# A third expert with a fixed place in a streamed mixture of experts, and overflow rounds that load through one buffer of their own

## The chip, the cores and the metric

The kernel runs on one core of a Trainium2 chip. The metric is the device time of one execution, in microseconds. Below, TensorE is PE, VectorE is DVE, ScalarE is ACT, GpSimd is POOL, and SyncE, which here only issues DMAs, is SP; "SPq" or "PEq" is the sequencer of an engine, which runs its branches, register loads and DMA issues.

## The reference

A decoder trunk of two layers on 256 tokens of width 1024, in float32. Each layer is an attention block (layer 0: two groups of sparse heads; layer 1: latent attention beside sliding-window attention) and then a top-2 mixture of 16 experts of hidden width 512. Each block is normalised and modulated by a vector from `c`. A final RMSNorm follows. The part that the change touches is the mixture of experts:

```
for each token: the router picks 2 of 16 experts and their weights w
y[token] = sum over its 2 experts e of  w * ( silu(h @ gate[e]) * (h @ up[e]) ) @ down[e]
x = x + gate_vector * y
```

`gate[e]` and `up[e]` are 1024 x 512, `down[e]` is 512 x 1024. One expert's weights are 6 MB, those of one layer 96 MB.

## The kernel before

**Groups.** The 16 experts of a layer are worked through in seven groups of 128 slots (`GROUPS`). A group holds two or three places, and a place is one to three blocks of 32 slots for one expert. PE multiplies 128 slots at a time, so a group costs it about the same whether it has two or three experts, but a group of three loads 18 MB and one of two 12 MB. `(0, 3)` means place 0 with 96 slots. Experts 14 and 15 have fixed places in group 0. The other 14 experts are put into places 0 to 13 by their token count (`RANKS`, `SORTED`): the fullest experts go to the widest places. The result of this sort is `ex_p`, a row of expert numbers on the chip.

**Loads.** Every expert's gate, up and down matrices come as two loads of 1 MB each (gate 2, up 2, down 2), all issued on SP, 96 in a layer. They go into 15 buffers of 1 MB: a ring of 10 (`slot`) and 5 more that are free in this part of the program (`room`); a buffer is free again when PE has done its last matmul from it. Each SP load uses one of eight semaphores in turn and waits for the load eight before it, so at most eight are in flight. `load_both` loads group 0 (L1185), `load_experts` the other groups (L1171). From group 1 on, SP first reads the expert's number from `ex_p` into a register (`load_value`, L1349), so no load of a sorted expert is issued before the sort is done. At that point 12 buffers hold four loads of the modulation weights and the eight gate and up loads of group 0, and three buffers are empty.

**Order.** For each group the loop calls `hidden` (loads gate and up, and multiplies), then `rows` of the group before it (loads its down and multiplies), then the gathering of the next group's tokens. So PE's order, and SP's, is gate and up of group i, down of group i-1, gate and up of group i+1.

**Overflow.** Tokens that don't fit their expert's place are done in extra rounds of 64 slots, up to seven, ahead of group 3 (`rest`, `round_`). A nest of conditions (`tc.If(n >= i + 1)`, L1453) skips the rounds that aren't needed. PE, ACT, DVE and SP take part in this nest. A round's six loads go on SP into six of the ring's slots, which `rest` withholds from the stream. Since SP is held by the nest, the twelve loads of group 3 are issued on POOL's own queue (`self.after`), and group 2's down is loaded ahead of the nest. In the profiled execution no instruction of a round ran.

At the ends of the nest SP has eight UNCONDITIONAL_BRANCH, and seven of them wait for the eight load semaphores, that is for nearly all loads in flight.

Of the kernel before, what the change touches and what calls it, by code (L numbers as in the profile page):

```python
# [10 lines left out]
F32 = mybir.dt.float32  # L11
# [6 lines left out]
ET = mybir.EngineType  # L18
# [3 lines left out]
S, D, P = 256, 1024, 128  # L22
NE, DE = 16, 512
CAP = 64
# [3 lines left out]
RING, EXTRA = 10, 5  # L28


GROUPS = [[(14, 2), (15, 2)], [(0, 3), (1, 1)], [(2, 2), (3, 1), (4, 1)], [(5, 2), (6, 2)], [(7, 2), (8, 1), (9, 1)],
          [(10, 2), (11, 2)], [(12, 2), (13, 2)]]
RANKS = 0, 9, 1, 10, 11, 2, 3, 4, 12, 13, 5, 6, 7, 8
SORTED = len(RANKS)
BLOCK = 32

# [71 lines left out]
def trunk(ctx, tc, ins, out):  # L108
    nc = tc.nc
    mm, vec, act, pool, sp = nc.tensor.matmul, nc.vector, nc.scalar, nc.gpsimd, nc.sync  # L110
# [28 lines left out]
    def slot(n_k, n):  # L139

        tag = order.pop(0)
        order.append(tag)
        t = room() if tag == "wx" else ring.tile([P, 2048], F32, tag="w", name="slot")
        return t[:, :n_k * n].rearrange("p (k f) -> p k f", k=n_k)
# [822 lines left out]
    def moe(cp, wk, layer, norm, end):  # L967
# [9 lines left out]
        for t in range(2):  # L977
            at = slice(t * P, (t + 1) * P)
# [179 lines left out]
            split_rows(v, yg, vec)  # L1158
            return [yg[:, 0], yg[:, 1]]

        def load_experts(nm, experts, k, tiles=None, queue=sp, fine=False):

            out = [[] for _ in experts]
            for h in range(2):
                for i, e in enumerate(experts):
                    t = tiles.pop(0) if tiles else slot(4, 512)
                    v = ins[nm][layer][bass.ds(e, 1)].rearrange("o (p k) f -> p (o k) f", k=k)
                    n = k // 2
                    t = t.rearrange("p a b -> p (a b)").rearrange("p (k f) -> p k f", k=n)
                    if not (fine and h):  # L1170
                        queue.dma_start(t, v[:, n * h:n * h + n, :])  # L1171
                    out[i].append((t, n))
            for k0 in range(0, n if fine else 0, 2):
                for x, e in zip(out, experts):
                    v = ins[nm][layer][bass.ds(e, 1)].rearrange("o (p k) f -> p (o k) f", k=k)
                    queue.dma_start(x[1][0][:, k0:k0 + 2, :], v[:, n + k0:n + k0 + 2, :])
            return [Rows(x) for x in out]

        def load_both(nm, e0):
# [31 lines left out]
        class Group:  # L1211


            def __init__(self, i, o, XG, c0):
                self.first, self.last = i == 0, (layer, i) == (1, len(GROUPS) - 1)
                self.after = i == 3
                self.o, self.XG, self.c0 = o, XG, c0
                self.p0, self.n = GROUPS[i][0][0], len(GROUPS[i])
                self.parts = blocks(GROUPS[i])
                first = sum(len(g) for g in GROUPS[:i])  # L1220
                self.owner = const("owner")[:, first:first + self.n]
                es = list(range(self.p0, self.p0 + self.n))
                if i:
                    es = [load_value(ex_p[:, e:e + 1], [(ET.SP, ET.Pool)[self.after]], NE - 1) for e in es]
                self.es = es
                self.Wd = None

            def hidden(self):
                names = ("moe_w_gate", "moe_w_up")
                if self.first:  # L1230
                    W = [load_both(nm, self.p0) for nm in names]
                else:
                    W = [load_experts(nm, self.es, 8, queue=(sp, pool)[self.after], fine=self.last and nm == names[1])
                         for nm in names]
                self.hid = gate_up(self.XG, self.c0, self.parts, *W)

            def slots(self):
                self.OT = wk.tile([P, 2, P], F32R, tag="OT", name="OT")
# [12 lines left out]
            def load_down(self):  # L1251
                if self.Wd is not None:
                    return
                if not self.last:
                    self.Wd = load_experts("moe_w_down", self.es, 4, queue=(sp, pool)[self.after])
                    return

                src = [ins["moe_w_down"][layer][bass.ds(e, 1)].rearrange("o (p k) f -> p (o k) f", k=4) for e in self.es]
                self.Wd = []
                for sl, step in zip(end.pieces, (2, 4, 2)):  # L1260
                    n = sl.stop - sl.start
                    if n == 512:
                        tiles = [slot(4, n) for _ in range(2)]
                    else:
                        tile_ = slot(8, n)
                        tiles = [tile_[:, 0:4], tile_[:, 4:8]]
                    for k in range(0, 4, step):
                        for t, v in zip(tiles, src):
                            sp.dma_start(t[:, k:k + step], v[:, k:k + step, sl])
                    self.Wd.append(tiles)  # L1270
# [31 lines left out]


        NR = 7
        w_x = cp.tile([P, 1], F32, name="w_x")
        OT_x = cp.tile([P, 2, 2, P], F32R, name="OT_x")
        sides = [slice(0, 64), slice(64, 128)]

        def x_hidden(XG, W):
            hid = XG.rearrange("p k s -> p (k s)")[:, 0:256]  # L1310
            g, u = bank("mm", [P, 256]), bank("sc", [P, 256])
            for w, b in zip(W, (g, u)):
                for k in range(8):
                    for h, at in enumerate(sides):
                        mm(b[at], XG[:, k, :], w[k][:, 256 * h:256 * h + 256], start=k == 0, stop=k == 7)
            act.activation(hid, g, AF.Silu)
            vec.tensor_tensor(hid, u, hid, ALU.mult)
            return hid
# [18 lines left out]
        def x_down(hT, Wd):  # L1337
            v, yg = row_tiles()
            y = bank("o", [P, 512])
            for k in range(4):  # L1340
                for h, at in enumerate(sides):
                    mm(y[at], hT[:, k, :], Wd[k][:, 512 * h:512 * h + 512], start=k == 0, stop=k == 3)
            for h, at in enumerate(sides):
                vec.scalar_tensor_tensor(v[at], y[at], w_x[at], gate[at, 512 * h:512 * h + 512], ALU.mult, ALU.mult)
            split_rows(v, yg, vec)
            return [lambda h=h: combine(OT_x[:, h], [yg[:, 0], yg[:, 1]], slice(512 * h, 512 * h + 512)) for h in range(2)]

        def load_value(at, engines, top):
            _, v = nc.values_load_multi_w_load_instructions(  # L1349
                at, engines=engines, min_val=0, max_val=top, skip_runtime_bounds_check_because="sums of indicators")  # L1350
            return v[0]
# [34 lines left out]
        def rounds():  # L1386
# [42 lines left out]
                of(at_x[:, t], pos[:, t])  # L1429
            vec.tensor_tensor(at_x, at_x, skip.unsqueeze(1).to_broadcast([P, 2, NR]), ALU.subtract)  # L1430

        def round_(i, space, o, XG):

            e = load_value(ex_x[:, i:i + 1], [ET.SP], NE - 1)
            tiles = list(space)
            W = [load_experts(nm, [e], 8, tiles)[0] for nm in ("moe_w_gate", "moe_w_up")]
            Wd, = load_experts("moe_w_down", [e], 4, tiles)
            pick(o, at_x[:, :, i:i + 1].to_broadcast([P, 2, 2]), CAP)
            gather(XG, CAP, o)
            hid = x_hidden(XG, W)  # L1440
            x_slots(o, wt_x[:, :, i:i + 1])
            for f in x_down(x_transposed(XG, hid), Wd):
                f()

        def rest():
            space = [slot(4, 512) for _ in range(6)]
            o = pick_tile()[:, :, 0:2 * CAP]
            XG = hp.tile([P, 8, CAP], F32, tag="HT", name="XG")
            n = load_value(ex_x[:, NR:NR + 1], [ET.PE, ET.Activation, ET.DVE, ET.SP], NR)

            def go(i):
                if i < NR:
                    with tc.If(n >= i + 1):  # L1453
                        round_(i, space, o, XG)
                        go(i + 1)
            go(0)

# [6 lines left out]
        for i in range(len(GROUPS)):  # L1464
            p = Group(i, o, XG, 128 * (i > 0 and i % 2 == 0))
            if i == 3:
                before.load_down()
                flush()
                rest()
            if p.last:  # L1470
                end.load()
            p.hidden()
            if before is not None:
                before.rows()
            p.slots()
            p.turn()
            if i % 2 == 0 and i < 5:
                o, XG = gathered(*then)
            elif i < 5:
                then = picked([i + 2, i + 3], placed[:, 0:2])  # L1480
            if i == 0:
                rounds()
            flush()
            before = p
# [293 lines left out]
```

## Time and profile before

| | us |
|---|---|
| median of 3 runs (lowest to highest) | 868.07 (867.78 to 868.67) |
| profiled execution | 869.42 |
| its span on the core | 867.2 |
| PE busy | 746.6 (86%) |
| DVE busy | 377.8 (44%) |
| ACT busy | 237.4 (27%) |
| POOL busy | 115.6 (13%) |
| DMA traffic | 291.14 MB, mean 336 GB/s |

The profile lists the busy time of each engine, of which PE has the most, and the mean rate of DMA. The rate is not even: the page's row of 40 slices shows 415 to 422 GB/s in most slices of the two expert parts (about 233 to 468 us and 620 to 850 us) and 96 to 387 in the attention parts. The views used below are windows (busy time, granted clock and DMA rate of a stretch), waits (what an engine waited for), timelines of an engine, the chain of waits that ended last, and DMA issues with their time from issue to landing.

### The profile page before, as it was taken

Reading aid. Unit: us, or ns where it says so; the run is one execution under the profiler, and the core shown is the slowest. Engines: PE = TensorE matmul, PEld = TensorE weight load, DVE = VectorE, ACT = ScalarE, POOL = GpSimd, SP = SyncE. Lnnn points to the kernel's source line nnn. Section 1 sums busy time; section 2 is a strip of 40 time slices with the busy share of each in tenths; the row PEclk is TensorE's granted clock in tenths of the full one; section 3 lists DMA queues with packets and bytes.
Section 4 is the critical chain, followed back from the end, with each engine's and each line's share of the span. In section 5 each row is a group of like instructions: output and inputs, shape, how many; then the busy total and the mean of one; then the engine's idle time right before and its main releaser. Section 6 shows DMA issues by size and latency. Waiting matters only on the chain. (4 is left out here: it accounts for less than half of the span.)

```text
span 867.2 us, 12251 instructions
## 1 busy us (share of the span) xinstructions
PE 746.6 (86%) x4499; PEld 381.9 (44%) x4499; DVE 377.8 (44%) x1091; ACT 237.4 (27%) x569; POOL 115.6 (13%) x118
## 2 busy tenths in 40 slices
PE   4699999999799969759997899979899967769996
PEld 1298765557443332214332568556443322214233
DVE  2285777767831231103206654876912031103214
ACT  1254545545311010001112454545111010002012
POOL 2020111233100001000011223344000001000001
PEclk9699999999699999879999999988699988979998
DMA  9999878796299998999999997733499989999992
GB/s 328 349 328 387 321 248 217 280 376 219 96 422 418 419 417 337 419 420 419 419 415 389 360 350 196 288 130 122 179 419 419 419 361 395 420 420 419 416 396 77
DMA packets 84840, 291.14 MB, mean 336 GB/s; under 512 B 9174, under 2 KB 23202, under 8 KB 63010
## 3 DMA queue, kind: packets, MB, share of 16 engines
q1 hardware_dynamic: 76976, 258.36, 77.9%
q0 software_dynamic: 4608, 29.37, 8.3%
q10 hardware_dynamic: 3186, 2.51, 0.9%
q8 instruction: 39, 0.64, 0.3%
q14 instruction: 31, 0.25, 0.1%
HBM read 289.16 MB, written 1.06 MB: 335 GB/s over the span
## 5 line engine op out<-in xcount | busy, mean ns | idle before, releaser
L1084 PE MATMUL o<-slot,hT 128*32 128x512 f32 (+2 forms) x448 | 93.5, 619 | 14.0 <-PEq L1453 13.1
L1084 PE MATMUL sc<-slot,XG 128*64 128x512 f32 (+1 forms) x416 | 92.1, 646 | 13.6 <-DMA slot<-in_moe_w_up_dram 13.6
L1111 DVE TENSOR_TENSOR hq<-sc,hid 128x512 f32<-128x512 f32 x14 | 14.7, 1049 | 184.3 <-PE sc L1084 184.3
L1084 PE MATMUL mm<-slot,XG 128*32 128x512 f32 (+1 forms) x416 | 85.9, 624 | 5.2 <-DMA slot<-in_moe_w_gate_dram 5.2
L507 ACT CAST hl<-slot 128x512 fp32r<-128x512 f32 (+2 forms) x112 | 60.7, 557 | 72.8 <-PE mm L524 45.8
L464 POOL TENSOR_TENSOR hl<-slot,hl 128x512 fp32r<-128x512 f32 x40 | 53.2, 1333 | 163.1 <-ACT hl L507 135.7
L1084 PE MATMUL mm<-room,XG 128*64 128x512 f32 (+1 forms) x224 | 57.1, 629 | 5.6 <-DMA room<-in_moe_w_gate_dram 5.6
L1084 PE MATMUL o<-room,hT 128*32 128x512 f32 (+2 forms) x208 | 58.6, 603 | 2.0 <-DMA room<-in_moe_w_down_dram 2.0
L1155 DVE SCALAR_TENSOR_TENSOR adac<-o,w,GATE 128x512 f32<-128x512 f32 (+1 forms) x29 | 21.2, 732 | 82.5 <-PE o L1084 81.5
L522 PE MATMUL mm<-HH,hl 128*128 128x256 f32 x176 | 54.5, 311 | 2.3 <-ACT HH L496 2.3
L1084 PEld LDWEIGHTS sc<-slot,XG 128*64 128x64 f32 (+1 forms) x416 | 25.3, 132 | 70.1 <-issue 48.6
L1137 ACT CAST yg<-adac 128x512 fp32r<-128x512 f32 (+1 forms) x28 | 17.1, 612 | 140.0 <-DVE adac L1155 140.0
L332 PE MATMUL tp<-slot,csil 128*32 128x512 f32 x344 | 49.2, 648 | 4.4 <-DMA slot<-in_ada_w_dram 4.2
L1084 PE MATMUL sc<-room,XG 128*32 128x512 f32 (+1 forms) x224 | 45.0, 656 | 8.3 <-DMA room<-in_moe_w_up_dram 8.3
L1068 ACT ACTIVATE XG<-tp,mod,mod 128x256 f32<-128x256 f32 (+1 forms) x32 | 17.2, 538 | 124.0 <-PE tp L1066 124.0
L524 PE MATMUL mm<-HH,hl 128*128 128x256 f32 x176 | 50.0, 286 | 0.6 <-DVE hl L464 0.6
L523 PE MATMUL mm<-HH,hl 128*128 128x256 f32 x176 | 50.4, 287 | 0.1
L1084 PEld LDWEIGHTS o<-slot,hT 128*32 128x32 f32 (+1 forms) x448 | 25.5, 125 | 54.3 <-issue 36.0
L464 DVE TENSOR_TENSOR hl<-slot,hl 128x512 fp32r<-128x512 f32 (+2 forms) x72 | 42.6, 611 | 15.3 <-ACT hl L507 15.0
L1066 PE MATMUL tp<-pick,XH 128*128 128x256 f32 (+1 forms) x128 | 41.9, 347 | 4.0 <-DVE XG L1070 2.6
L1145 DVE TENSOR_TENSOR X<-X,tp 128x512 f32<-128x512 f32 (+1 forms) x56 | 36.0, 675 | 16.5 <-PE tp L1144 16.2
L1144 PE MATMUL tp<-yg,OT 128*128 128x512 f32 (+1 forms) x112 | 36.6, 431 | 7.5 <-ACT yg L1137 3.5
(377 smaller groups left out, 1305.9 us busy)
## 6 DMA issues: line engine op xcount, KB each, us to landing
slot<-in_ada_w_dram SPq DMA_DIRECT2D x43, 1024.0 KB, 10.3
slot<-in_moe_w_gate_dram SPq DMA_DIRECT2D x37, 1024.0 KB, 15.1
slot<-in_moe_w_down_dram SPq DMA_DIRECT2D x35, 1024.0 KB, 19.7
slot<-in_moe_w_up_dram SPq DMA_DIRECT2D x34, 1024.0 KB, 18.6
room<-in_moe_w_up_dram SPq DMA_DIRECT2D x20, 1024.0 KB, 16.8
room<-in_moe_w_gate_dram SPq DMA_DIRECT2D x19, 1024.0 KB, 15.2
room<-in_moe_w_down_dram SPq DMA_DIRECT2D x17, 1024.0 KB, 18.8
slot<-in_ev_w_in_dram SPq DMA_DIRECT2D x8, 1024.0 KB, 9.5
```

The lines of the kernel that those rows point to most:

```text
L332: mm(b[g:g + 32], csil[:, k, 1 - half:33 - half], W[k], start=k < 4, stop=k >= 4)
L464: eng.tensor_tensor(lo, v, hi.bitcast(F32), ALU.subtract)
L507: act.copy(hi, src)
L522: mm(o, a[0], b[0], start=start, stop=False, skip_group_check=True)
L523: mm(o, a[0], b[1], start=False, stop=False, skip_group_check=True)
L524: mm(o, a[1], b[0], start=False, stop=stop, skip_group_check=True)
L1066: mm(b, xk[i][:, t, k, :], o[:, t, 0:n], start=t == i == 0, stop=t == i == 1)
L1068: act.activation(XG[:, k, :], b, AF.Identity, bias=sh[:, k:k + 1], scale=fa[:, k:k + 1])
L1084: last[0] = mm(*args, **kw)
L1144: mm(cb, OT[:, t, :], x, start=i == 0, stop=i == 1)
L1145: vec.tensor_tensor(X[:, t, sl], X[:, t, sl], cb, ALU.add)
L1155: vec.scalar_tensor_tensor(v, y, w, gate[:, sl], ALU.mult, ALU.mult)
```

## The change

- `GROUPS` and `RANKS`: expert 13 now has a fixed place too, in group 1, beside the one sorted place 12; 13 experts are sorted. Groups of three experts are now groups 2 and 4 as before; groups 1, 3, 5 and 6 have two. Each group has as many loads as before (12, 12, 18, 12, 18, 12, 12).
- `load_mixed` (L1247) loads group 1: the two gate halves and the first up half of expert 13 are issued ahead of the read of `ex_p`, into the three empty buffers; then the sorted expert's gate, and the rest of up.
- An overflow round takes no ring slots. Its six loads go one after another through one tile (`space`) of a pool in which `XG` had a buffer, on POOL's queue (`streamed`); `XG_x` is a small tile of its own. POOL takes SP's part in the nest.
- Group 3's loads go on SP like all others, and group 2's down is loaded after group 3's gate and up, in the loop's own order.

```diff
-GROUPS = [[(14, 2), (15, 2)], [(0, 3), (1, 1)], [(2, 2), (3, 1), (4, 1)], [(5, 2), (6, 2)], [(7, 2), (8, 1), (9, 1)],
-          [(10, 2), (11, 2)], [(12, 2), (13, 2)]]
+GROUPS = [[(14, 2), (15, 2)], [(12, 2), (13, 2)], [(0, 2), (1, 1), (2, 1)], [(3, 3), (4, 1)], [(5, 2), (6, 1), (7, 1)],
+          [(8, 2), (9, 2)], [(10, 2), (11, 2)]]
...
-                if i:
-                    es = [load_value(ex_p[:, e:e + 1], [(ET.SP, ET.Pool)[self.after]], NE - 1) for e in es]
+                self.mixed = i == 1
+                if self.mixed:
+                    self.parts = self.parts[::-1]
+                elif i:
+                    es = [load_value(ex_p[:, e:e + 1], [ET.SP], NE - 1) for e in es]
...
+            def load_mixed(self, gate_, up):
...
+                g1, u1 = [half(gate_, e1, 0), half(gate_, e1, 1)], [half(up, e1, 0)]
+                e0 = self.es[0] = load_value(ex_p[:, self.p0:self.p0 + 1], [ET.SP], NE - 1)
+                g0 = [half(gate_, e0, h) for h in range(2)]
+                u1.append(half(up, e1, 1))
+                u0 = [half(up, e0, h) for h in range(2)]
...
+        def streamed(nm, e, k, space):
...
+            for h in range(2):
+                t = space.rearrange("p (k f) -> p k f", k=n)
+                pool.dma_start(t, v[:, n * h:n * h + n, :])
+                for i in range(n):
+                    yield t[:, i, :]
...
         def rest():
-            space = [slot(4, 512) for _ in range(6)]
+            space = hp.tile([P, 2048], F32, tag="HT", name="space")
             o = pick_tile()[:, :, 0:2 * CAP]
-            XG = hp.tile([P, 8, CAP], F32, tag="HT", name="XG")
-            n = load_value(ex_x[:, NR:NR + 1], [ET.PE, ET.Activation, ET.DVE, ET.SP], NR)
+            n = load_value(ex_x[:, NR:NR + 1], [ET.PE, ET.Activation, ET.DVE, ET.Pool], NR)
...
             if i == 3:
-                before.load_down()
                 flush()
                 rest()
```

SP at the sort, in layer 0. TENSOR_LOAD `ex_p` is the read of the sort's result, ISA a register instruction; `DMAHW4_49` and the like are the load semaphores. Before:

```order
L1185 DMA slot<-in_moe_w_up_dram 128x2x1024 [waits DMAHW2_49]
L1185 DMA slot<-in_moe_w_up_dram 128x2x1024 [waits DMAHW3_49]
L1349 TENSOR_LOAD ex_p [waits PE_49,DVE_49,Activation_49,Pool_49]
L1171 ISA
L1171 DMA slot<-in_moe_w_gate_dram 128x2048 [waits DMAHW4_49]
```

After:

```order
L1185 DMA slot<-in_moe_w_up_dram 128x2x1024 [waits DMAHW2_49]
L1185 DMA slot<-in_moe_w_up_dram 128x2x1024 [waits DMAHW3_49]
L1247 DMA slot<-in_moe_w_gate_dram 128x2048 [waits DMAHW4_49]
L1247 DMA slot<-in_moe_w_gate_dram 128x2048 [waits DMAHW5_49,DVE_49,Pool_49]
L1247 DMA slot<-in_moe_w_up_dram 128x2048 [waits DMAHW6_49,DVE_49,Pool_49]
L1369 TENSOR_LOAD ex_p [waits PE_49,DVE_49,Activation_49,Pool_49]
```

Three loads have moved ahead of the read, and wait for no sort.

SP at the end of the nest, in layer 0, ahead of the first load that follows it. Before:

```order
L1453 UNCONDITIONAL_BRANCH
L1453 UNCONDITIONAL_BRANCH [waits SP_sequencer_49,DMAHW2_49,DMAHW3_49,DMAHW4_49,DMAHW5_49,DMAHW6_49,DMAHW7_49]
L1453 UNCONDITIONAL_BRANCH [waits SP_sequencer_49,DMAHW0_49,DMAHW1_49,DMAHW2_49,DMAHW3_49,DMAHW4_49,DMAHW5_49,DMAHW6_49,DMAHW7_49] x6
L1349 TENSOR_LOAD ex_p
L1171 ISA
L1171 DMA room<-in_moe_w_gate_dram 128x2048 [waits DMAHW4_49,DMAHW2_49,DMAHW6_49,DMAHW0_49,PE_49]
```

After, between group 3's gate and up loads:

```order
L1171 DMA slot<-in_moe_w_gate_dram 128x2048 [waits DMAHW2_49,PE_49]
L1171 ISA
L1171 DMA slot<-in_moe_w_gate_dram 128x2048 [waits DMAHW3_49,PE_49]
L1479 UNCONDITIONAL_BRANCH
L1171 ISA
L1171 DMA slot<-in_moe_w_up_dram 128x2048 [waits DMAHW4_49,PE_49]
```

The nest is gone from SP; one unconditional branch without a wait is left in the stream of loads.

PE behind the nest, in layer 0 (`o` is a down product, `mm` a gate product, `hT` and `XG` the slots' activations). Before:

```order
L1453 UNCONDITIONAL_BRANCH [waits PE_49] x7
L1084 MATMUL o<-slot,hT 32x512 [waits DMAHW2_49,DVE_49,PE_49]
L1084 MATMUL o<-slot,hT 32x512 [waits DMAHW1_49]
L1084 MATMUL o<-slot,hT 32x512 [waits DMAHW0_49]
L1084 MATMUL o<-slot,hT 32x512
```

After:

```order
L1479 UNCONDITIONAL_BRANCH [waits PE_49] x7
L1084 MATMUL mm<-slot,XG 32x512 [waits DMAHW1_49,PE_49,Activation_49]
L1084 MATMUL mm<-slot,XG 32x512 [waits DMAHW0_49]
L1084 MATMUL mm<-slot,XG 32x512 x14
L1084 MATMUL mm<-slot,XG 32x512 [waits DMAHW3_49]
```

PE's own nest stays where it was; behind it now comes group 3's gate, where group 2's down stood.

## Rows read from the trace of the kernel before

**Rows 1.** Windows of all engines: stretch, busy us (x instructions) each, PEclk, DMA share, GB/s.
```profile
220.00:230.00 10.00, 5.56 (x16) 2.92 (x17) 8.87 (x34) 1.81 (x3) 1.00 (x1) 0.66 0.01 2
230.00:240.00 10.00, 10.00 (x39) 6.80 (x40) 9.52 (x51) 1.83 (x4) 0.00 (x0) 0.50 0.71 271
...
325.00:332.00 7.00, 7.00 (x48) 1.95 (x51) 0.49 (x2) 0.00 (x0) 2.01 (x4) 0.71 0.46 156
332.00:339.00 7.00, 7.00 (x46) 2.38 (x40) 2.30 (x5) 1.13 (x3) 0.64 (x2) 1.00 1.01 426
395.00:441.00 46.00, 44.12 (x238) 16.97 (x239) 13.45 (x24) 7.32 (x14) 0.21 (x1) 1.00 1.01 420
...
610.00:620.00 10.00, 8.52 (x34) 6.47 (x35) 9.57 (x42) 0.92 (x2) 0.00 (x0) 0.62 0.11 19
...
711.00:718.00 7.00, 7.00 (x52) 2.06 (x48) 0.00 (x0) 0.00 (x0) 2.26 (x5) 0.73 0.49 163
```

**Rows 2.** Waits of SP's sequencer, 195 to 350 us: us in total, times, longest.
```profile
SPq L1171 <- PE mm L1084: 28.1, 8, 8.2
SPq L1453 <- SPq L1453: 27.0, 7, 5.3
SPq L1349 <- DVE ex_p L1378: 21.6, 1, 21.6
```

**Rows 3.** Timeline of SP's issues, both layers, around the sort: start, us, issues.
```profile
231.94 1.91 SPq L1171 DMA_DIRECT2D slot<-in_moe_w_gate_dram  x3
...
617.98 1.87 SPq L1171 DMA_DIRECT2D slot<-in_moe_w_gate_dram  x3
```

**Rows 4.** The same around the nest, both layers.
```profile
300.85 0.33 SPq L1171 DMA_DIRECT2D room<-in_moe_w_down_dram  x1
329.38 0.33 SPq L1171 DMA_DIRECT2D room<-in_moe_w_gate_dram  x1
...
686.77 0.33 SPq L1171 DMA_DIRECT2D room<-in_moe_w_down_dram  x1
715.19 1.30 SPq L1171 DMA_DIRECT2D room<-in_moe_w_gate_dram  x2
```

**Rows 5.** Instructions of line L1453: ns min/median/max, first and last start.
```profile
L1453 SPq COMPARE_BRANCH  x2: 50/50/50, 301.6 to 687.5; - x2
...
L1453 PEldq COMPARE_BRANCH  x2: 6131/6292/6452, 318.1 to 703.8; - x2
```

**Rows 6.** PE's timeline in layer 1, groups 0 and 1: start, us, operation.
```profile
621.67 9.23 PE L1084 MATMUL mm<-slot,XG 128*64 128x512 f32 x32
...
647.43 1.06 PE L1084 MATMUL mm<-slot,XG 128*32 128x512 f32 x8
...
651.75 3.62 PE L1084 MATMUL sc<-room,XG 128*32 128x512 f32 x32
655.18 3.62 PE L1084 MATMUL sc<-slot,XG 128*32 128x512 f32 x32
```

**Rows 7.** Waits of PE in layer 1, 703.9 to 862.5 us: us in total, times, longest.
```profile
PE sc L1084 <- DMA slot<-in_moe_w_up_dram: 10.6, 3, 6.7
...
PE mm L1084 <- DMA room<-in_moe_w_gate_dram: 5.6, 2, 4.3
```

**Rows 8.** The chain that ended last, layer 1: start, us, what.
```profile
740.55 30.74 DMA slot<-in_moe_w_up_dram
...
837.29 6.18 PE o L1084 x28
```

**Rows 9.** PE's timeline, last down product of layer 0: start, us, operation [idle before, releaser].
```profile
464.34 0.64 PE L1084 MATMUL o<-room,hT 128*64 128x512 f32 x1 [1.08 <-DMA room<-in_moe_w_down_dram]
...
467.40 0.59 PE L1084 MATMUL o<-slot,hT 128*64 128x512 f32 x1
```

**Rows 10.** DMA issues, 195 to 345 us: tile, queue, count, KB each, median us to landing.
```profile
slot<-in_moe_w_down_dram SPq DMA_DIRECT2D x8, 1024.0 KB, 19.9
...
slot<-in_moe_w_gate_dram POOLq DMA_DIRECT2D x1, 1024.0 KB, 7.3
```

More of the change, by code (lines that the diff above doesn't have):

```diff
@@ L28 @@
 RING, EXTRA = 10, 5
-GROUPS = [[(14, 2), (15, 2)], [(0, 3), (1, 1)], [(2, 2), (3, 1), (4, 1)], [(5, 2), (6, 2)], [(7, 2), (8, 1), (9, 1)],
-          [(10, 2), (11, 2)], [(12, 2), (13, 2)]]
-RANKS = 0, 9, 1, 10, 11, 2, 3, 4, 12, 13, 5, 6, 7, 8
+GROUPS = [[(14, 2), (15, 2)], [(12, 2), (13, 2)], [(0, 2), (1, 1), (2, 1)], [(3, 3), (4, 1)], [(5, 2), (6, 1), (7, 1)],
+          [(8, 2), (9, 2)], [(10, 2), (11, 2)]]
+RANKS = 1, 8, 9, 0, 10, 2, 11, 12, 3, 4, 5, 6, 7
 SORTED = len(RANKS)
@@ L1159, in rows_of, with load_experts @@
             return [yg[:, 0], yg[:, 1]]
-        def load_experts(nm, experts, k, tiles=None, queue=sp, fine=False):
+        def load_experts(nm, experts, k, fine=False):
             out = [[] for _ in experts]
@@ L1165, in load_experts @@
                 for i, e in enumerate(experts):
-                    t = tiles.pop(0) if tiles else slot(4, 512)
+                    t = slot(4, 512)
                     v = ins[nm][layer][bass.ds(e, 1)].rearrange("o (p k) f -> p (o k) f", k=k)
@@ L1170, in load_experts @@
                     if not (fine and h):
-                        queue.dma_start(t, v[:, n * h:n * h + n, :])
+                        sp.dma_start(t, v[:, n * h:n * h + n, :])
                     out[i].append((t, n))
@@ L1175, in load_experts @@
                     v = ins[nm][layer][bass.ds(e, 1)].rearrange("o (p k) f -> p (o k) f", k=k)
-                    queue.dma_start(x[1][0][:, k0:k0 + 2, :], v[:, n + k0:n + k0 + 2, :])
+                    sp.dma_start(x[1][0][:, k0:k0 + 2, :], v[:, n + k0:n + k0 + 2, :])
             return [Rows(x) for x in out]
@@ L1215, in __init__ @@
                 self.first, self.last = i == 0, (layer, i) == (1, len(GROUPS) - 1)
-                self.after = i == 3
                 self.o, self.XG, self.c0 = o, XG, c0
@@ L1231, in hidden, with half @@
                     W = [load_both(nm, self.p0) for nm in names]
-                else:
-                    W = [load_experts(nm, self.es, 8, queue=(sp, pool)[self.after], fine=self.last and nm == names[1])
-                         for nm in names]
+                elif self.mixed:
+                    W = self.load_mixed(*names)
+                else:
+                    W = [load_experts(nm, self.es, 8, fine=self.last and nm == names[1]) for nm in names]
                 self.hid = gate_up(self.XG, self.c0, self.parts, *W)
+            def load_mixed(self, gate_, up):
+                e1 = self.es[1]
+                def half(nm, e, h):
+                    t = slot(4, 512)
+                    sp.dma_start(t, ins[nm][layer][bass.ds(e, 1)].rearrange("o (p k) f -> p (o k) f", k=8)[:, 4 * h:4 * h + 4, :])
+                    return t, 4
+                g1, u1 = [half(gate_, e1, 0), half(gate_, e1, 1)], [half(up, e1, 0)]
[3 more added lines that the diff above has]
+                u0 = [half(up, e0, h) for h in range(2)]
+                return [Rows(g0), Rows(g1)], [Rows(u0), Rows(u1)]
             def slots(self):
@@ L1254, in load_down @@
                 if not self.last:
-                    self.Wd = load_experts("moe_w_down", self.es, 4, queue=(sp, pool)[self.after])
+                    self.Wd = load_experts("moe_w_down", self.es, 4)
                     return
@@ L1304, in moe @@
         NR = 7
+        XG_x = cp.tile([P, 8, CAP], F32, name="XG_x")
         w_x = cp.tile([P, 1], F32, name="w_x")
@@ L1312, in x_hidden @@
             for w, b in zip(W, (g, u)):
-                for k in range(8):
+                for k, row in enumerate(w):
                     for h, at in enumerate(sides):
-                        mm(b[at], XG[:, k, :], w[k][:, 256 * h:256 * h + 256], start=k == 0, stop=k == 7)
+                        mm(b[at], XG[:, k, :], row[:, 256 * h:256 * h + 256], start=k == 0, stop=k == 7)
             act.activation(hid, g, AF.Silu)
@@ L1339, in x_down @@
             y = bank("o", [P, 512])
-            for k in range(4):
+            for k, row in enumerate(Wd):
                 for h, at in enumerate(sides):
-                    mm(y[at], hT[:, k, :], Wd[k][:, 512 * h:512 * h + 512], start=k == 0, stop=k == 3)
+                    mm(y[at], hT[:, k, :], row[:, 512 * h:512 * h + 512], start=k == 0, stop=k == 3)
             for h, at in enumerate(sides):
@@ L1430, in rounds @@
             vec.tensor_tensor(at_x, at_x, skip.unsqueeze(1).to_broadcast([P, 2, NR]), ALU.subtract)
+        def streamed(nm, e, k, space):
+            v = ins[nm][layer][bass.ds(e, 1)].rearrange("o (p k) f -> p (o k) f", k=k)
+            n = k // 2
+            for h in range(2):
[3 more added lines that the diff above has]
+                    yield t[:, i, :]
         def round_(i, space, o, XG):
[L1434 to L1437, printed above, removed]
+            e = load_value(ex_x[:, i:i + 1], [ET.Pool], NE - 1)
             pick(o, at_x[:, :, i:i + 1].to_broadcast([P, 2, 2]), CAP)
             gather(XG, CAP, o)
-            hid = x_hidden(XG, W)
+            hid = x_hidden(XG, [streamed(nm, e, 8, space) for nm in ("moe_w_gate", "moe_w_up")])
             x_slots(o, wt_x[:, :, i:i + 1])
-            for f in x_down(x_transposed(XG, hid), Wd):
+            for f in x_down(x_transposed(XG, hid), streamed("moe_w_down", e, 4, space)):
                 f()
         def rest():
-            space = [slot(4, 512) for _ in range(6)]
+            space = hp.tile([P, 2048], F32, tag="HT", name="space")
             o = pick_tile()[:, :, 0:2 * CAP]
-            XG = hp.tile([P, 8, CAP], F32, tag="HT", name="XG")
-            n = load_value(ex_x[:, NR:NR + 1], [ET.PE, ET.Activation, ET.DVE, ET.SP], NR)
+            n = load_value(ex_x[:, NR:NR + 1], [ET.PE, ET.Activation, ET.DVE, ET.Pool], NR)
             def go(i):
@@ L1453, in go @@
                     with tc.If(n >= i + 1):
-                        round_(i, space, o, XG)
+                        round_(i, space, o, XG_x)
                         go(i + 1)
```

## The prediction, on record before the changed kernel ran

> **What bounds the kernel now.** I read the windows first. In an expert part the DMA engines are busy all the time and move 420 GB/s (395 to 441 us), while PE is busy 44.1 of 46 us [rows 1]. A load is 1,048,576 bytes, so it takes 2.50 us of this stream. After the sort each layer has 88 of its 96 loads still to move: 88 x 2.5 = 220 us, twice, which is half of the span. The stream is the bound, but PE stands close behind, and two places interrupt the stream.
>
> The first is the sort. Between 220 and 230 us the DMA engines move 2 GB/s, and in layer 1 19 GB/s between 610 and 620 [rows 1]. SP's waits say why: 21.6 us for `ex_p` [rows 2]. The first load behind it is issued at 231.94 and 617.98 [rows 3]. The window 230 to 240 moved 271 GB/s, that is 6.5 us at 420, so the stream of layer 0 starts at 233.5; by the same lag of 1.6 to 2 us that of layer 1 starts at about 620.0.
>
> The second is the nest. SP's compare and branch itself takes 50 ns [rows 5], but SP then waits 27.0 us in seven waits at L1453 for its own loads [rows 2]: it issues nothing from 300.85 to 329.38 and from 686.77 to 715.19 [rows 4]. Loads in flight and POOL's few carry the stream over most of that; the windows 325 to 332 and 711 to 718 then show 156 and 163 GB/s, with 426 behind the first [rows 1]. The holes cost 7 x (1 - 156/420) = 4.4 and 7 x (1 - 163/420) = 4.3 us of stream.
>
> **The change, part by part.** Times are those of the profiled execution (869.42 us, span 867.2), which is 1.35 us above the median of 868.07; the difference that the sum gives is taken from the median.
>
> *Early loads.* Three loads move from behind the sort to ahead of it, where DMA is nearly idle. They need 3 x 2.5 = 7.5 us, and SP has 21.6 us there [rows 2], so they delay nothing. Behind the sort 85 loads are left: -7.5 us per layer.
>
> *What they take.* They fill the three empty buffers, which before held the first loads behind the sort. Now loads 1 to 4 behind the sort go into the modulation's four buffers, 5 to 12 into group 0's eight, and load 13 needs one that group 1 has released. PE's timeline of layer 1 shows group 0's gate at 621.67, four buffers in 9.23 us (2.3 us each, near the stream's 2.5), so loads 5 to 12 find room. Group 1's gate halves end at 648.4 and 651.8, and its first up half at 655.2 [rows 6]. The unhindered stream would want loads 13 to 15 landed at 620.0 + 13 x 2.5 = 652.5, 655.0 and 657.5; issued at those releases, with 2 us to start and 2.5 to move, they land at 652.9, 656.3 and 659.7. The last is 2.2 late: I take +2.5 us per layer. The bounds are 0 (buffers come in time) and 7.5 (everything that was loaded early is lost again).
>
> *The nest leaves SP.* The drain goes, -4.4 and -4.3 us. SP keeps one unconditional branch that waits for nothing. What hides it is the loads in flight: one takes 19.9 us from issue to landing [rows 10]. PE's skip of the nest stays, 6.1 and 6.5 us [rows 5]; it is covered as long as PE has slack behind the stream. If not, it shows as PE time and not as DMA time.
>
> The row shows that PE's taken branch costs 6.1 to 6.5 us and SP's 50 ns, with the same nest to skip [rows 5]. [...]
>
> *Group 3 on SP's queue, no slots withheld.* The same bytes on one queue in place of two: 0 us for the stream. What moves is which load comes first. With both queues busy, an up load took 30.74 us [rows 8] against 19.9 [rows 10], and PE waited 10.6 and 5.6 us for weights behind the nest [rows 7]. These 16.2 us are PE idle time that can go; they are the limit of what layer 1 can gain while PE's work is unchanged. The order behind PE's nest, gate of group 3 ahead of down of group 2, has the same matmuls: 0 us, between +1 and -1 for the buffers that it releases earlier or later. DVE makes three selections ahead of group 1 and four ahead of group 3, the other way round than before, and is busy 13.45 of 46 us in the middle of the stream [rows 1]: 0.
>
> *Sum, layer 1.* The last load that group 5's down needs is the 92nd of 96, so the 81st behind the sort; with half a megabyte for the final norm's row it is through at 620.0 + 81.5 x 2.5 + 2.5 = 826.3, landed at about 827. In the chain this product starts at 837.29 and its second half, which needs that load, at 837.29 + 3.1 = 840.4 [rows 8]. PE without its 16.2 us of waits would be there at 824.2, so the stream still decides, by about 3 us. Gain 840.4 - 827 = 13.4, less 0.5 for the small delays that no row prices: 12.9.
>
> *Sum, layer 0.* The last down needs all 85 loads and 1 MB of another kind: 233.5 + 86 x 2.5 + 2.5 = 451.0, landed at 451.8. From there 467.99 - 464.34 = 3.65 us of matmuls, so 455.4 in place of 467.99 [rows 9]: 12.6. But the same count for before gives 233.5 + 89 x 2.5 + 4.4 + 0.8 = 461.2, and PE waited for this load until 464.34 [rows 9]: 3.1 us that the count doesn't explain. I let half of it stay: 12.6 - 1.6 = 11.0. The attention of layer 1 then starts that much earlier, with its own weights behind the same stream, so the gain is carried on.
>
> Together 23.9 us: 868.07 - 23.9 = 844.2 (845.5 for a profiled execution).
>
> **The rivals.**
>
> *The early loads buy nothing.* Buffers, not bytes, pace the stream after the sort: PE runs at half clock there (window 230 to 240: 0.50 [rows 1]), and every buffer filled early is one less for the stream. For it: SP waited 28.1 us for PE's releases in eight waits [rows 2]. Against it: the stream still ran at 420. The bubble is then 7.5 and not 2.5, 2 x 5 us worse: 854.2.
>
> *Neither bubble nor unexplained lag.* Buffers come in time and the 3.1 us of layer 0 go with the two queues: 15.1 in layer 0, and layer 1 ends on PE's limit, 16.2: 868.07 - 31.3 = 836.8.
>
> *The nest still stops the stream.* POOL's part in the nest or SP's branch leaves a hole as large as today's. For it: PE's 6.1 to 6.5 us [rows 5]. Against it: no wait for loads is left on SP. That is 4.4 + 4.3 lost again: 852.9.
>
> *Slower: an overflow round runs.* Places have other sizes: the ninth-fullest expert, before in a place of 64, now has 32 slots, and expert 13 a fixed 64. If any count exceeds its place, one round runs with its six loads one after another through one tile: 6 x 7.3 (a load alone on POOL's queue [rows 10]) = 44 us in which PE waits, where before the loads overlapped. One round in one layer gives 844 + 44 = 888. It decides from a 33rd token of the ninth expert or a 65th of expert 13. Against it: worked out from the reference's own inputs, the ninth counts are 26 and 20, expert 13 has 26 and 23, and the fullest has 58 and 71 (96 slots), so no round runs; in the execution of before none ran.
>
> **How the numbers follow.** Forecast 0.70, early loads buy nothing 0.10, no bubble and no lag 0.10, nest still stops the stream 0.05, slower 0.05. With the ends of the unknown terms (bubble 0 to 2.5, the full lag kept in both layers: 7.5 + 4.35 - 2.5 = 9.35 each, so 849.4) and the two rivals at 836.8 and 854.2, the range is 836.5 to 854.5. About 0.2% (1.7 us) is what a measurement of this kernel can tell from no change. All cases but the last are faster by more than that; I leave 0.02 for several costs adding up to nothing: faster 0.93, same 0.02, slower 0.05.
>
> **What would show it.** Three loads of SP ahead of the read of `ex_p`, landing while DMA is idle, and the stream starting as late as now; one dip of about 2.5 us of stream some 30 us behind the sort; no window near the nest under 400 GB/s; SP without waits for its own loads there; PE's branch still some 6 us; the two waits of PE for up and gate weights behind the nest gone or short; layer 0's last down near 452, group 5's last down half about 13 us earlier against the sort of layer 1's start. I would be wrong if the stream keeps its pace but the end doesn't follow: then PE, with its branch and its half-clock stretches, is the bound earlier than the 3 us of slack in layer 1 suggest. I would also be wrong if loads behind the sort wait for buffers much longer than 2.5 us.

## The result and the profile after

The changed kernel takes 848.45 us (848.29 to 849.8, four runs), the kernel before 867.92 us beside it: a ratio of 0.9778, interval 0.9761 to 0.9795, or 19.5 us less. The forecast was 844.2 in a range of 836.5 to 854.5: the way and the range hold, but only 19.5 of 23.9 us came. The profiled execution spans 848.1 us, against 867.2.

The windows of the kernel after, in the columns of [rows 1], around layer 0's sort, behind it, at the nest, and the same in layer 1:

```profile
220.00:230.00 10.00, 6.04 (x19) 3.39 (x19) 8.81 (x35) 1.32 (x3) 0.52 (x1) 0.62 0.01 2
230.00:240.00 10.00, 10.00 (x38) 6.51 (x39) 9.42 (x50) 1.83 (x4) 0.00 (x0) 0.52 0.76 294
...
260.00:270.00 10.00, 10.00 (x50) 3.62 (x50) 0.00 (x0) 1.16 (x2) 0.00 (x0) 1.00 0.90 324
...
320.00:330.00 10.00, 5.60 (x36) 1.66 (x40) 0.76 (x2) 0.00 (x0) 0.00 (x0) 0.66 1.01 413
330.00:340.00 10.00, 10.00 (x94) 3.35 (x90) 0.17 (x2) 0.97 (x2) 0.00 (x0) 1.00 1.01 418
...
610.00:620.00 10.00, 10.00 (x35) 5.13 (x36) 9.16 (x49) 1.15 (x3) 0.00 (x0) 0.58 0.99 383
...
640.00:650.00 10.00, 10.00 (x50) 3.31 (x48) 0.00 (x0) 0.65 (x2) 0.00 (x0) 1.00 0.84 292
...
700.00:710.00 10.00, 5.26 (x28) 1.53 (x32) 0.76 (x2) 0.00 (x0) 0.00 (x0) 0.52 1.01 414
```

Three things are to be seen. The stream still has nothing to move ahead of the sort's end (2 GB/s). The nest no longer makes a hole: 413, 418 and 414 GB/s where before fell to 156 and 163. And a new gap stands some 30 us behind the sort: 324 and 292 GB/s. In loads' time it is 10 x (1 - 324/420) = 2.3 us in layer 0 and 10 x (1 - 292/420) = 3.0 us in layer 1.

SP's timeline shows the three early loads, the sort, and the gap's cause (`x5` between 249.56 and 269.23 are five issues with waits between them):

```profile
202.13 1.07 SPq L1247 DMA_DIRECT2D slot<-in_moe_w_gate_dram  x2
205.72 0.33 SPq L1247 DMA_DIRECT2D slot<-in_moe_w_up_dram  x1
231.44 0.96 SPq L1247 DMA_DIRECT2D room<-in_moe_w_gate_dram  x2
...
249.56 19.67 SPq L1171 DMA_DIRECT2D slot<-in_moe_w_gate_dram  x5
269.44 0.86 SPq L1171 DMA_DIRECT2D room<-in_moe_w_up_dram  x2
```

SP's waits, 195 to 350 us, answer to [rows 2]. There SP waited 28.1 us for PE's gate products, 8.2 at most, and 27.0 for itself at the nest; the second line is gone and the first has grown to 40.0 and 11.0, because SP now comes to its buffers earlier than PE frees them:

```profile
SPq L1171 <- PE mm L1084: 40.0, 9, 11.0
SPq L1369 <- DVE ex_p L1398: 21.5, 1, 21.5
```

The nest on the engines that still go through it, in the columns of [rows 5]:

```profile
L1479 POOLq COMPARE_BRANCH  x2: 45/49/53, 238.5 to 616.0; - x2
...
L1479 PEldq COMPARE_BRANCH  x2: 5927/6049/6171, 318.2 to 698.2; - x2
```

PE's stall is as long as before; POOL's is 49 ns. PE's waits behind the nest in layer 1 answer to [rows 7]: the 10.6 and 5.6 us for up and gate weights are gone, and 1.0 us for a down load is the only wait for DMA that is left.

```profile
PE mm L1084 <- PEq L1479: 6.3, 1, 6.3
...
PE o L1084 <- DMA slot<-in_moe_w_down_dram: 1.0, 1, 1.0
```

The chain that ended last shows that the stream decides the end of layer 1 now; before, the chain's last load landed at 771.3 [rows 8]:

```profile
762.92 16.76 DMA slot<-in_moe_w_down_dram
779.81 21.02 DMA slot<-in_moe_w_gate_dram
800.98 14.92 DMA slot<-in_moe_w_down_dram
816.04 7.94 PE o L1084 x28
```

### The profile page after: what moved, and what is told of

Read it like the earlier page. It is cut to its first block, busy times and chain, and to the rows that moved or that the text cites. A ratio compares the mean times of both kernels' runs of the same rounds, so it can differ in the third digit from the quotient of the medians.

```text
span 848.1 us, 12220 instructions
## 1 busy us (share of the span) xinstructions
PE 748.2 (88%) x4499; PEld 387.2 (46%) x4499; DVE 377.8 (45%) x1095; ACT 237.1 (28%) x569; POOL 101.6 (12%) x94
## 3 DMA queue, kind: packets, MB, share of 16 engines
HBM read 289.16 MB, written 1.06 MB: 342 GB/s over the span
## 5 line engine op out<-in xcount | busy, mean ns | idle before, releaser
L1084 PE MATMUL mm<-slot,XG 128*32 128x512 f32 (+1 forms) x464 | 111.2, 656 | 12.6 <-PEq L1479 12.6
L1084 PE MATMUL sc<-slot,XG 128*32 128x512 f32 (+1 forms) x344 | 72.1, 592 | 0.0
L1084 PEld LDWEIGHTS mm<-slot,XG 128*32 128x32 f32 (+1 forms) x464 | 28.3, 131 | 72.4 <-issue 70.7
L1084 PE MATMUL sc<-room,XG 128*32 128x512 f32 (+1 forms) x296 | 60.7, 593 | 0.0
L1084 PE MATMUL o<-room,hT 128*64 128x512 f32 (+2 forms) x176 | 51.7, 615 | 4.6 <-DMA room<-in_moe_w_down_dram 4.6
L1084 PE MATMUL mm<-room,XG 128*32 128x512 f32 (+1 forms) x176 | 54.0, 708 | 0.0
L1144 PE MATMUL tp<-yg,OT 128*128 128x512 f32 (+1 forms) x112 | 38.7, 448 | 11.1 <-DVE X L1145 5.2
```

Source lines behind the costliest of these rows:

```text
L1084: last[0] = mm(*args, **kw)
L1144: mm(cb, OT[:, t, :], x, start=i == 0, stop=i == 1)
```

## The experiments

The theory was that of the prediction: each load that starts in the idle time ahead of the sort saves 2.5 us per layer; the third is paid back by the gap, because it takes a free buffer; and the nest on SP cost 4.4 us per layer. The main rivals were that the early loads buy nothing, that the whole gain is that of the nest, and that PE is the bound already.

**Early loads undone, first attempts.** Three kernels moved the read of `ex_p` ahead of three, one and two of expert 13's loads, in the order of the code:

```diff
-                g1, u1 = [half(gate_, e1, 0), half(gate_, e1, 1)], [half(up, e1, 0)]
                 e0 = self.es[0] = load_value(ex_p[:, self.p0:self.p0 + 1], [ET.SP], NE - 1)
+                g1, u1 = [half(gate_, e1, 0), half(gate_, e1, 1)], [half(up, e1, 0)]
```

> The changed kernel with the read of the sort's result moved ahead of expert 13's three loads; the same loads in the same order otherwise. My theory (three loads less behind the sort, -7.5 us, paid back in part by a gap of 2.3 to 3.1 us in the stream some 30 us later, as the windows of the changed kernel show): 2 x 4.8 = 9.6 us slower than the changed kernel's 848.4, so 858.0 (856.5 to 859.5), and no gap in the windows 260 to 270 and 640 to 650 us. Rival 'the early loads buy nothing': 848.4. Rival 'the gap costs nothing at the end': 848.4 + 15 = 863.4.

> The changed kernel with two of expert 13's loads ahead of the read instead of three. My theory of the gap (the load that finds no free buffer has to wait for group 1's matmuls): one load more behind the sort (+2.5 us) but a gap of about 1 instead of 2.3 to 3.1, so +0.8 us per layer: 850.0 (848.5 to 851.5). Rival (the gap is not from the buffers and stays): +2.5 per layer, 853.4.

> The changed kernel with one of expert 13's loads ahead of the read. My theory: +5.0 us for two loads, less the whole gap of 2.3 to 3.1: +2.3 per layer, 853.0 (851.5 to 854.5). Rival (the gap stays): +5 per layer, 858.4.

Measured: 848.47 us (848.16 to 849.34; ratio 0.9778, 0.976 to 0.9796), 847.87 (0.9771, 0.9751 to 0.9791) and 848.56 (0.9773, 0.9756 to 0.9791). That looks like the first rival, but the timeline of the first shows that the edit did not do what it says:

```profile
202.48 1.02 SPq L1247 DMA_DIRECT2D slot<-in_moe_w_gate_dram  x2
206.05 0.33 SPq L1247 DMA_DIRECT2D slot<-in_moe_w_up_dram  x1
231.56 0.96 SPq L1247 DMA_DIRECT2D room<-in_moe_w_gate_dram  x2
```

The loads still start at 202 us, and the first load that needs the sort's result comes behind them, at 231.56. In the other two kernels all three loads start by 206.4 us as well. The loads depend on nothing in the sort, and the line that they stand on did not set SP's order. So the three are repeats of the changed kernel, and decide nothing; they say that its time repeats within 0.7 us.

**Early loads undone, second attempt.** Expert 13's number was copied on DVE into the row of the sort's result, all three loads (or the third alone) reading it from there:

```diff
                     vec.tensor_copy(ex_p[:, 0:n], placed[0:1, 5, 0:n])
+                    vec.tensor_copy(ex_p[:, n:16], route[0:1, 5, n:16])
...
+                e1 = load_value(ex_p[:, self.p0 + 1:self.p0 + 2], [ET.SP], NE - 1)
                 g1, u1 = [half(gate_, e1, 0), half(gate_, e1, 1)], [half(up, e1, 0)]
```

> The changed kernel with no load ahead of the sort: expert 13's number is copied by one small DVE instruction beside the sort's result and read from there, so that its three loads stand behind the read on SP. My theory (7.5 us less behind the sort, of which a gap of 2.3 to 3.1 is given back): 2 x 4.8 = 9.6 us slower than the changed kernel's 848.4, so 858.0 (856.5 to 859.5), without the gap in the windows 260 to 270 and 640 to 650 us. Rival 'the early loads buy nothing': 848.4 to 849.4. Rival 'the gap costs nothing at the end': 863.4.

> The changed kernel with two loads ahead of the sort and the third behind the read, by the same small copy. My theory of the gap (the first load that finds no free buffer waits for group 1's matmuls): one load more behind the sort (+2.5 us), the gap shrinks from 2.3 to 3.1 us to about 1: +0.8 us per layer, 850.0 (848.5 to 851.5). Rival (the gap is not from the buffers and stays): +2.5 per layer, 853.4.

Measured: 847.26 us (846.54 to 847.59; 0.9759, 0.9734 to 0.9785) and 848.85 (847.6 to 849.45; 0.9773, 0.9745 to 0.98). Again a row spoils the reading:

```profile
214.58 0.99 SPq L1247 DMA_DIRECT2D slot<-in_moe_w_gate_dram  x2
215.84 0.33 SPq L1247 DMA_DIRECT2D slot<-in_moe_w_up_dram  x1
```

The copied number is known before the sort, so the loads start some 12 us later than in the change (214.58 for 202.13), and still 17 us ahead of the first load behind the sort, at 231.41. The runs show one thing: the early loads may start as late as 214.6 us, well ahead of the sort's end at 231, at no loss. (The first of the two lies 1.2 us under the change, which the intervals don't separate.)

**Early loads undone, with a number that depends on the sort:**

```diff
                     vec.tensor_copy(ex_p[:, 0:n], placed[0:1, 5, 0:n])
+                    vec.scalar_tensor_tensor(ex_p[:, n:n + 1], placed[0:1, 5, n - 1:n], 0.0, route[0:1, 5, n:n + 1],
+                                             ALU.mult, ALU.add)
```

> The changed kernel with no load ahead of the sort: expert 13's number is now computed from the sort's result (one small DVE instruction behind it, about 0.1 us), so that its three loads cannot start before the sort ends. My theory (7.5 us less behind the sort, of which a gap of 2.3 to 3.1 is given back): 9.6 us slower than the changed kernel's 848.4, so 858.0 (856.5 to 860), near nest_only, whose groups alone differ; no gap in the windows 260 to 270 and 640 to 650 us. Rival 'the early loads buy nothing': 848.4 to 849.4.

> The changed kernel with two loads ahead of the sort and the third made to depend on the sort's result. My theory of the gap (the first load that finds no free buffer waits for group 1's matmuls): +2.5 us for the third load, the gap shrinks from 2.3 to 3.1 us to about 1, +0.8 us per layer: 850.0 (848.5 to 851.5). Rival (the gap is not from the buffers and stays): +2.5 per layer, 853.4.

> The changed kernel with one load ahead of the sort and two made to depend on its result. My theory: +5.0 us for two loads, less the whole gap of 2.3 to 3.1: +2.3 per layer, 853.0 (851.5 to 854.5). Rival (the gap stays): +5 per layer, 858.4.

Measured:

| loads ahead of the sort | us | ratio to before, interval |
|---|---|---|
| 0 | 859.17 (857.61 to 860.56) | 0.990, 0.9854 to 0.9945 |
| 1 | 854.6 (854.47 to 856.6) | 0.9861, 0.9815 to 0.9906 |
| 2 | 849.15 (848.3 to 849.94) | 0.9787, 0.9743 to 0.983 |
| 3 (the change) | 848.45 (848.29 to 849.8) | 0.9778, 0.9761 to 0.9795 |

The first load gives 4.6 us, the second 5.4, the third 0.7; 2 x 2.5 = 5.0 is what a load saves in two layers. So the first two pay in full and the third is given back. That is the theory, with one size off: with two loads ahead it left a gap of about 1 us in each layer, and the windows below show none. With one load ahead the time lies 0.1 us above the range expected, the other two lie inside. The kernel without early loads starts its loads behind the sort, and its windows show that the gap goes with them:

```profile
231.78 1.00 SPq L1247 DMA_DIRECT2D slot<-in_moe_w_gate_dram  x2
```

```profile
260.00:270.00 10.00, 10.00 (x50) 3.60 (x48) 0.15 (x1) 1.16 (x2) 0.00 (x0) 1.00 1.01 420
...
640.00:650.00 10.00, 10.00 (x53) 4.26 (x53) 1.09 (x2) 2.00 (x4) 0.00 (x0) 1.00 1.01 418
```

With two loads ahead the same windows are full too, which is why the third buys nothing:

```profile
260.00:270.00 10.00, 10.00 (x48) 3.31 (x47) 0.00 (x0) 1.08 (x2) 0.00 (x0) 1.00 1.01 421
...
640.00:650.00 10.00, 10.00 (x48) 3.30 (x45) 0.00 (x0) 0.60 (x1) 0.00 (x0) 1.00 1.01 420
```

**Each half of the change alone.** One kernel is before with the new groups and `load_mixed`, the nest left on SP; the other is the changed kernel with the old groups and no fixed third expert. The edit of the second, against the changed kernel, is shown here; its `RANKS` go back too:

```diff
-GROUPS = [[(14, 2), (15, 2)], [(12, 2), (13, 2)], [(0, 2), (1, 1), (2, 1)], [(3, 3), (4, 1)], [(5, 2), (6, 1), (7, 1)],
-          [(8, 2), (9, 2)], [(10, 2), (11, 2)]]
+GROUPS = [[(14, 2), (15, 2)], [(0, 3), (1, 1)], [(2, 2), (3, 1), (4, 1)], [(5, 2), (6, 2)], [(7, 2), (8, 1), (9, 1)],
+          [(10, 2), (11, 2)], [(12, 2), (13, 2)]]
...
-                self.mixed = i == 1
+                self.mixed = False
```

> The kernel before with the new groups and expert 13's three early loads alone; the nest stays on SP and withholds six slots, group 3 loads on POOL. My theory: 2 x 4.8 us = 9.6 less than before's 868.1, so 858.5 (857 to 861). Rival 'the early loads buy nothing': 868. Rival 'the whole gain comes from the early loads': 849.

> The kernel before with the nest moved off SP alone: rounds streamed through one tile on POOL, no slots withheld, group 3's loads on SP; the old groups, 14 sorted experts, no early load. My theory: the two holes of 4.4 and 4.3 us go, and up to 1 us per layer from the waits of PE on the shared queues: 858.4 to 859.4. Rival 'the whole gain comes from the nest': 849. Rival 'the nest's hole is covered anyway': 868.

Measured: 856.5 us with the early loads alone (855.07 to 858.68; 0.9868, 0.9837 to 0.99), and 859.82 with the nest alone (855.92 to 860.73; 0.989, 0.9854 to 0.9926), beside 867.82 for before. That is 11.3 and 8.0 us, together 19.3 of the 19.5. The first is 0.5 us under the range expected, the second 0.4 above it. The hole is in the first kernel's windows and not in the second's (first fence: early loads alone; second: nest alone):

```profile
320.00:330.00 10.00, 7.62 (x52) 2.28 (x56) 0.76 (x2) 0.00 (x0) 2.63 (x5) 0.66 0.68 258
```

```profile
320.00:330.00 10.00, 5.87 (x18) 2.00 (x20) 0.76 (x2) 0.00 (x0) 0.00 (x0) 0.66 1.01 414
```

The nest alone (859.82) and the changed kernel with no load ahead (859.17) differ by the groups, the order of group 1's loads and one small DVE instruction: the new groups as such are worth nothing that can be measured.

The second kernel undoes three things together: SP's part in the nest, the withheld slots and the second queue. In before, POOL too stood still at the nest. Its next load of group 3 goes into a withheld slot and waits 17.45 us for SP's end of the nest, so SP and POOL go on at the same time, 329.4 us:

```profile
329.33 0.53 POOL L1171 DMA_DIRECT2D slot<-in_moe_w_gate_dram  x1 [17.45 <-SPq L1453]
```

So both SP's drain and the withheld slots held the stream; no run separates them.

**PE's stall at the nest.** The call of `rest()` is left out, and with it the rounds:

```diff
                 flush()
-                rest()
```

> The changed kernel without the call of rest(): the overflow rounds and the nest of conditions that skips them are left out, on every engine. PE's 6.3 us stall at the nest goes in both layers. My theory (the stream of loads sets the end, PE's stall lies beside it): 0 to 2 us less, so 846.4 to 848.4. Rival (PE is already the bound behind the nest, so that its stall counts): 3 to 6 us per layer less, so 836.4 to 842.4.

Measured: 849.04 us (847.09 to 850.07; 0.9786, 0.9769 to 0.9804). PE is spared 6.3 us in each layer, and the time stays. Its waits in layer 1 say where they went:

```profile
PE o L1084 <- DMA slot<-in_moe_w_down_dram: 4.8, 3, 3.8
...
PE sc L1084 <- DMA slot<-in_moe_w_up_dram: 3.8, 1, 3.8
...
PE sc L1084 <- DMA room<-in_moe_w_up_dram: 1.5, 1, 1.5
```

PE comes earlier and waits 10.1 us for loads where it waited 1.0. The stall lay beside the stream. (The median is 0.6 us above what was expected, less than the spread of its runs.)

**The end of layer 0.** In the changed kernel a 1 MB load of layer 1's bias rows, on POOL's queue, falls among layer 0's last down loads. Here it is issued on SP, behind the first weights of the attention, where the change issued it at 435.79 us:

```diff
-        pool.dma_start(BM, bass.AP(scr.tensor, 0, [[1, P], [384, 8], [1, 256]]))
+        queue.dma_start(BM, bass.AP(scr.tensor, 0, [[1, P], [384, 8], [1, 256]]))
...
-        BMR, BM = bias_rows(big)
+        BMR, BM = bias_rows(big, sp)
```

> The changed kernel with the 1 MB load of layer 1's bias rows issued on SP behind the attention's weights, instead of on POOL in the middle of layer 0's last down loads. It tests whether layer 0's end still hangs on the stream: if it does, the last downs land 2.5 us earlier and layer 0 ends up to 2.5 us earlier, 845.9 to 847; if the attention's first weights are on the same stream and set its start, the 2.5 us come back there and it stays at 848.4.

Measured: 844.1 us (843.55 to 845.02; 0.9734, 0.9691 to 0.9778), faster than both kernels: by the medians 4.35 us under the change, where 2.5 was the most expected; its slowest run (845.02) is faster than the fastest of the change (848.29). The end of layer 0 shows most of it. Each kernel has three fences: PE's timeline; SP's first load that waits for the last down load, which tells when that one landed; and a window with the granted clock (the third number from the end). The changed kernel:

```profile
449.65 0.61 PE L1084 MATMUL o<-room,hT 128*64 128x512 f32 x1 [2.35 <-DMA room<-in_moe_w_down_dram]
...
452.27 1.12 PE L1084 MATMUL o<-room,hT 128*64 128x512 f32 x1
...
453.18 1.06 PE L1084 MATMUL o<-room,hT 128*64 128x512 f32 x1
...
456.02 3.60 PE L1084 MATMUL o<-room,hT 128*64 128x512 f32 x16
...
464.12 2.35 PE L332 MATMUL tp<-slot,csil 128*32 128x512 f32 x20 [0.26 <-DVE X L1145]
```

```profile
455.42 4.59 SPq L187 DMA_DIRECT2D slot<-in_od_w_in_dram  x2
```

```profile
452.00:453.00 1.00, 1.00 (x3) 0.30 (x4) 0.83 (x2) 0.00 (x0) 0.00 (x0) 0.50 0.98 387
```

With the bias rows behind:

```profile
447.54 0.64 PE L1084 MATMUL o<-room,hT 128*64 128x512 f32 x1
...
449.69 0.64 PE L1084 MATMUL o<-room,hT 128*64 128x512 f32 x1
...
452.32 3.62 PE L1084 MATMUL o<-room,hT 128*64 128x512 f32 x16
...
460.41 2.78 PE L332 MATMUL tp<-slot,csil 128*32 128x512 f32 x24 [0.25 <-DVE X L1145]
```

```profile
452.30 9.00 SPq L187 DMA_DIRECT2D slot<-in_od_w_in_dram  x3
```

```profile
450.00:451.00 1.00, 1.00 (x6) 0.29 (x4) 0.61 (x2) 0.00 (x0) 0.00 (x0) 1.00 1.05 400
```

Two things have changed. The last down load lands at 452.3 in place of 455.4, 3.1 us earlier. And in the changed kernel PE waits 2.35 us for a load, after which the granted clock falls to 0.50 (452 to 454 us) and the matmuls that start there take 1.06 to 1.12 us each; with the bias rows behind, the wait is gone, the clock is 1.00 (450 to 460 us) and they take 0.59 to 0.64. From the first of these matmuls to the second half of the product it took 3.75 us (452.27 to 456.02), here 2.63 (449.69 to 452.32). But the second half needs the last load too, so of that only the time behind the landing counts, 456.02 - 455.4 = 0.6 us. Together the next block starts at 460.41 for 464.12, 3.7 us earlier.

Later weights of the attention now stand behind that 1 MB, and no loss shows there: the first load behind layer 1's sort comes at 602.93 for 609.32. Of these 6.4 us, 2.7 were gained in the attention, which no run explains; the profiled execution of the change was the slowest of its four. The edit moves the load in time and to another queue at once, and no run says which of the two counted.

## Why the prediction was right, and where it was short

*Early loads, -7.5 us per layer, and the gap, +2.5.* Right. The net of 2 x 5.0 = 10.0 us was measured as 859.17 - 848.45 = 10.7 inside the changed kernel, and as 11.3 with the rest of before; the gap as 2.3 and 3.0 us. The cause was named rightly as well: with two loads ahead there is no gap. What I did not draw from my own sum is that the third load was worthless: 3 x 2.5 - 2.5 is the same as 2 x 2.5.

*The nest leaves SP, -4.4 and -4.3 us.* Right in size: 8.0 us alone (ratio 0.989, 0.9854 to 0.9926), and no window shown at the nest is under 413 GB/s. That it was SP's drain alone, and not the withheld slots with it, is not shown. The unconditional branch left on SP stands between group 3's gate and up loads. Their issues follow each other closely, in layer 0:

```profile
290.64 3.46 SPq L1171 DMA_DIRECT2D slot<-in_moe_w_gate_dram  x4
294.33 0.33 SPq L1171 DMA_DIRECT2D slot<-in_moe_w_up_dram  x1
```

The gate loads are issued until 294.10, and the up load follows 0.23 us later (0.24 in layer 1): SP did not stall. PE's branch took 5.9 to 6.2 us again.

*PE's skip is covered.* Right, by the kernel without the nest.

*Layer 0's sum, 11.0 us.* This step was too large. PE reached layer 1's first weights at 464.12 in place of 472.46, 8.3 us earlier. Two terms were off. The 3.1 us which my count of before could not explain, and of which I let half go, stayed: the count for after, from the sum's start at 233.5, puts the last landing at 451.8, and it landed at 455.4, 3.6 us later. The stream's rate is about 0.9 us of this, 396 GB/s in place of 420 from 440 to 455.4 us; the rest is open. And I took PE's matmuls at full speed; in the changed kernel PE runs dry 2.35 us, the granted clock falls to 0.50, and the second half of the last product began at 456.02, 0.6 us behind the landing. The last experiment gave 3.7 us back by moving one 1 MB load, which I had counted at 2.5 us: 3.1 of them are the landing and 0.6 the clock.

*Layer 1's sum, 12.9 us.* From the first load behind the sort (617.98 before, 609.32 after) to the end of group 5's down (843.50 and 824.00) it took 225.5 and 214.7 us: 10.8 less. The count puts the last of its loads 207 us behind the stream's start, at about 610.9 + 207 = 817.9. PE waited for the second load of this product until 816.04, ran part of the first half at a granted clock of 0.50 (817 to 819 us), and began the second half, which needs the fourth load, at 821.19, 3.3 us after the sum's time. The fourth load was issued at 806.00. Its row (count, KB, us from issue to landing), PE's, and the window with the clock:

```profile
slot<-in_moe_w_down_dram SPq DMA_DIRECT2D x1, 1024.0 KB, 14.9
```

```profile
821.19 3.63 PE L1084 MATMUL o<-slot,hT 128*64 128x512 f32 x16
```

```profile
817.00:818.00 1.00, 1.00 (x4) 0.30 (x2) 0.00 (x0) 0.00 (x0) 0.00 (x0) 0.50 1.03 403
```

It landed at 820.9, 3.0 us behind the count, and the clock added the last 0.3. As in layer 0 the loads came later than the count at 420 GB/s, and the half clock was the small part.

*The sum.* 8.4 us at layer 0's last product, 0.3 in the attention behind it, 10.8 in layer 1, less 0.4 in the tail, make the 19.1 us between the spans. The mechanism was right in every part that a run tested; short were the ends of the two streams, by 2.6 and 2.1 us. The rows of before had shown this lag, as the 3.1 us. The prediction's own end of the range with the lag kept whole in both layers was 849.4, and 848.45 was measured.

*The rivals.* "The early loads buy nothing" and "the nest still stops the stream" are refuted by the table and the windows; "neither gap nor lag" falls, since both are there. No round ran, so what one costs was not tested; the 7.3 us from which the prediction priced it is not that of a load alone, since five more were issued within 3 us of it.

What stays open: why the last loads of both streams land 3.0 to 3.6 us behind the count, what share of the nest's 8.0 us the withheld slots had, and why the first of the early loads gave 4.6 us and the second 5.4; the intervals of these runs are wider than that.

## What to carry to other kernels

Loads that need no data-dependent number belong into the idle time ahead of the number, but each takes a buffer, so count to the first load that finds none: here the third was worth nothing. A condition on a queue that issues loads can cost what its end has to wait for, and not the branch: here the branch took 50 ns and the waits 27.0 us. Put the condition on an engine whose loads are not in flight: here that was worth 8.0 us, together with the slots and the second queue. And look at which small load falls among the last ones that a stage waits for: moving one megabyte was worth 4.35 us, as much as half of the nest.

## What the runs showed that was not expected

The order of the code did not set the order of SP's queue: five kernels that should have delayed loads left them early, since nothing they depended on was late. Check in the timeline that an edit moved what it was to move before its time is read.

One load of 1 MB among the last ones of a stage cost 3.7 us there, not 2.5: the last load landed 3.1 us later, and 0.6 us came from PE's clock, which was granted at 0.50 after a wait of 2.35 us, so that the matmuls took 1.06 to 1.12 us where the same ones take 0.59 at 1.00.

The unconditional branch that is left on SP cost 0.24 us at most, beside 5.9 to 6.2 us for PE's jump over the nest.
